# Opening stage on one load queue, small PSUM tiles in one bank, and last scalings in four products: a two-layer decoder trunk on one core

## The chip, the cores and the metric

One core of a Trainium2 chip runs the whole program. TensorE multiplies matrices and writes PSUM (8 banks), VectorE and ScalarE do elementwise work and reductions, GpSimd and SyncE here only issue DMAs; each engine works through its own queue in order. Sixteen DMA engines move the data. The metric is device time in microseconds of one execution; lower is better.

## What is computed

```python
def reference(x, c, ...):                       # x (1, 256, 1024), c (1, 1024), float32
    c_act = silu(c)
    for l in range(2):
        mod = c_act @ w_ada[l] + b_ada[l]       # nine vectors: sh0, sc0, g0, sh1, sc1, g1, sh2, sc2, g2
        h = rmsnorm(x, norm_g[l, 0]) * (1 + sc0) + sh0
        x = x + 0.5 * g0 * swiglu(h, ffn_w_gate[l, 0], ffn_w_up[l, 0], ffn_w_down[l, 0])   # 1024 -> 2816 -> 1024
        h = rmsnorm(x, norm_g[l, 1]) * (1 + sc1) + sh1
        x = x + g1 * token_mix(h, ...)          # gated MLP over chunks | differential attention | sparse attention
        h = rmsnorm(x, norm_g[l, 2]) * (1 + sc2) + sh2
        x = x + 0.5 * g2 * swiglu(h, ffn_w_gate[l, 1], ffn_w_up[l, 1], ffn_w_down[l, 1])
    return rmsnorm(x, final_g)
```

## The kernel before

All activations stay on the chip, transposed: `xT` holds 8 chunks (`KD`) of 128 features by 256 tokens. Every weight is used once and streamed from DRAM in float32. A product is made of three: each weight tile (`load`, L203, into the five buffers `wst`) is split into `wh` (ScalarE, L211) and `wl` = rest (VectorE, L215), each activation into a high and a low half, and TensorE (`mm`, L223) adds wh*high, wh*low and wl*high.

**The modulation vectors** come from `w_ada`: each `ast` tile (512 KB, four buffers `ad`) is multiplied by silu(c) (`crow`) and summed along its row by one VectorE instruction (L192 in `ada_sum`; L381 in the opening). GpSimd issues these loads (L181 in `ada_load`; L374), ahead of the stage that needs the vector.

**The opening** (`startup`, L363) is the first half-FFN's norm and its first seven gate and up tiles, with the loop over the 8 chunks k outside: for each k it loads and splits 1792 columns of weights in two parts (1024 and 768, `first`), makes this k's two modulation columns from two `ast` tiles (`ada_sum0`, L381 to L385), makes the chunk h[k] (`h_chunk`, L274: L276 VectorE, L279 ScalarE high half, L280 VectorE low half), and runs 42 products into seven PSUM banks `ps_fst`. Up to the first `h[0]` the order on TensorE, VectorE and ScalarE is written by hand (`manual_schedule`); the loop behind it is ordered by a planner that takes ready instructions by program order. The rest of the constant tables (`cst[:, P:]`, `par[:, npar0:]`, L443 and L444) and a small weight `w2` (L581) wait for no buffer.

**FFNs** (`ffn`, L447) run gate and up tiles in turn, then 8 down tiles. **The mixer** (`mix`, L547) issues its steps in the order of `MIX_ORDER`, by hand on TensorE alone; the step `a` of layer 0 sums two `ast` tiles and loads two more. `xs_in` (L591) holds both banks of pool `psw` for the token-major projections; `ws_in` (L323) takes its bank from `psw` too. The pool `pst` has one bank: `ps_cs` (compressed scores), `ps_ct` (their transposes), `ps_da` and the norm's sums take it in turn.

**The end**: after the last down tile the norm's factor per token is spread over partitions in PSUM (`rp`), eight VectorE instructions scale a chunk each by `final_g` and `rp` (L1036), and SyncE stores each (L1038).

Of the kernel before, what the change touches and what calls it, by code (L numbers as in the profile page):

```python
# [17 lines left out]
P = 128  # L18
# [32 lines left out]
k.1 dp.0 dp.1 ds.0 c.0 dx.0 k.0 ds.1 dx.1 c.1 v dr.0 q.0 ch dr.1 ns.0 a co do.0 do.1 nx.0 a cs.0 dn q.1 a q.2 go df ns.1  # L51
ct.0 nr.0 nx.1 a w.0.0.4 cs.2 no.0 q.3 a ns.2 nx.2 nr.1 ct.2 a cs.1 ns.3 nx.3 nr.2 cs.3 a ct.1 no.1 no.2 a nr.3 w.1.0.6
# [60 lines left out]
def trunk_kernel(ctx: ExitStack, tc: tile.TileContext, A, depth=DEPTH, nf=NF, fsplit=FSPLIT):  # L113
# [58 lines left out]
    last_wl = [None]  # L172
# [30 lines left out]
    def load(src, cols, pool=wst, tag="wst"):  # L203
        st = pool.tile([P, cols], F32, name="wst", tag=tag)
        nc.sync.dma_start(st, src)
        return st

    def split(src, cols, mid=None):
        st = load(src, cols)
        wh = whp.tile([P, cols], F32R, name="wh", tag="wh")  # L210
        nc.scalar.activation(wh, st, AF.Copy)  # L211
        if mid:
            mid()
# [114 lines left out]

    def add_out(l, s, m, ps, nxt, halves):
# [33 lines left out]
    def startup(ns):  # L363
# [3 lines left out]
        nc.gpsimd.dma_start(crow, A["crow"])  # L367
        b1 = sm.tile([P, KD], F32, name="b1", tag="b1", bufs=1)

        def ada_load0(k):  # L370
            sts = []
            for m in (1, 0):
                st = adp.tile([P, D], F32, name="ast", tag="ast")
                nc.gpsimd.dma_start(st, A["w_ada"][0, m, k])  # L374
                sts.append(st)
            return sts

        def ada_sum0(k, sts):
# [8 lines left out]
        def first(k, mid=None):  # L387
            parts = []
            for f0, f1 in ((0, (ns + 1) // 2), ((ns + 1) // 2, ns)):
                if f1 > f0:  # L390
                    src = A["w_first"][k, :, f0 * 2 * P:f1 * 2 * P]
                    parts.append((f0, f1, *split(src, 2 * (f1 - f0) * P, None if f0 else mid)))
            return parts

        with tc.manual_schedule(engines={mybir.EngineType.PE, mybir.EngineType.DVE, mybir.EngineType.Activation}):
# [8 lines left out]
            dma(cst[:, :P], A["cst"][:, :P])  # L404
            nc.vector.tensor_scalar_add(b1, lp(0, "bada")[:, KD:2 * KD], 1.0)
# [14 lines left out]
            ada_sum0(0, sts)  # L420
            rb = rms_bcast(rsqrt_tokens(st), in_psum=True)
            parts = first(0, lambda: h_chunk(0, 0, 0, rb))
        pss = []
        for f in range(ns):
            pool_, tag = (psm, "mm") if f < 5 else (psw, "w")
            pss.append(pool_.tile([P, 2 * T], F32, name="ps_fst", tag=tag))
        for k in range(KD):
            if k:
                parts = first(k)
            if k + 1 < KD:  # L430
                ada_sum0(k + 1, ada_load0(k + 1))
                h_chunk(0, 0, k + 1, rb)
            for f0, f1, wh, wl in parts:
                tiles = [(pss[f][:, e * T:(e + 1) * T], 2 * (f - f0) + e) for f in range(f0, f1) for e in range(2)]
                step = len(tiles) if k == 0 else 1
                for n0 in range(0, len(tiles), step):
                    for o, n in tiles[n0:n0 + step]:
                        s = slice(n * P, (n + 1) * P)
# [696 lines left out]
```

## Time and profile before

| | us |
|---|---|
| median of 3 runs | 1076.78 (1075.27 to 1077.12) |
| the profiled execution | 1076.35 |
| its span in the trace | 1074.4 |
| TensorE busy | 1028.0 |
| VectorE busy | 849.0 |
| ScalarE busy | 576.3 |

The span runs from the first to the last record of the execution; 1.95 us of the profiled execution's time lie around it. A busy time adds up an engine's instructions. TensorE's is modelled: its instructions overlap, so a busy stretch may still run slower than another, at a lower granted clock for example.

### The profile page before, as it was taken

To read this page: it belongs to the slowest core of one execution; us is meant where nothing else is said; L and a number is where in the kernel's file an instruction comes from. 1 tells how busy PE (TensorE), PEld (TensorE's weight loads), DVE (VectorE), ACT (ScalarE), POOL (GpSimd) and SP (SyncE) were. 2 spreads that over 40 slices of the span, in tenths; PEclk is the share of its full clock that TensorE was granted. 3 is DMA by queue.
4 is the path that set the end of the run, shared out by engine and by line. 5 is a ranking of instruction groups with operands and counts; after the bars stand their busy time and mean duration, and the time that the engine had idled before them with its cause. 6 is when DMAs were issued, how large, how long until landed. Compare 5 with 4: busy or idle time off the path is not lost.

```text
span 1074.4 us, 19840 instructions
## 1 busy us (share of the span) xinstructions
PE 1028.0 (96%) x7684; PEld 948.5 (88%) x7684; DVE 849.0 (79%) x1589; ACT 576.3 (54%) x1022; POOL 77.7 (7%) x151
## 2 busy tenths in 40 slices
PE   7789999999898999999999999999998999999997
PEld 5689998888676999998899999889786799999986
DVE  5689989989994899965679999667987489655553
ACT  4355544565576755444565544455566676444441
POOL 2101111000100022100001111000000001000000
PEclk8899999999999999999999999999998999999999
DMA  9899998947620499986658999765632057756551
GB/s 361 301 327 328 390 365 308 366 132 249 228 95 21 157 388 408 404 274 174 192 159 308 409 408 368 249 189 176 237 133 67 1 177 299 229 181 184 170 154 40
DMA packets 73967, 258.05 MB, mean 240 GB/s; under 512 B 8337, under 2 KB 9745, under 8 KB 73873
## 3 DMA queue, kind: packets, MB, share of 16 engines
q1 hardware_dynamic: 52560, 180.17, 48.7%
q0 software_dynamic: 20880, 76.03, 19.0%
q8 instruction: 60, 0.98, 0.4%
q10 hardware_dynamic: 432, 0.58, 0.2%
q14 instruction: 35, 0.28, 0.1%
HBM read 255.70 MB, written 1.05 MB: 239 GB/s over the span
## 4 chain that ended last, share of the span: by engine, by line
PE 77%; DVE 11%; DMA 6%; ACT 3%; issue 2%; POOL 0%; DVEq 0%; ACTq 0%; POOLq 0%; SPq 0%
PE ps_ws L223 42%; PE ps_dn L223 23%; PE ps_out L223 4%; PE ps_wu L223 4%; DVE wl L215 3%; DMA ast<-in_w_ada_dram 2%; PE ps_y L223 1%; DMA wst<-in_w_first_dram 1%; PE ps_s L223 1%; ACT pn L541 1%; DVE rt L515 1%; DVE mx L536 1%; DMA wst<-in_w_in_vs_dram 1%; ACT wh L211 1%; DVE h L280 1%
## 5 line engine op out<-in xcount | busy, mean ns | idle before, releaser
L211 ACT ACTIVATE wh<-wst 128x1024 fp32r<-128x1024 f32 (+2 forms) x332 | 342.0, 1032 | 360.7 <-issue 129.7
L215 DVE TENSOR_TENSOR wl<-wst,wh 128x1024 fp32r<-128x1024 f32 (+2 forms) x332 | 392.6, 1187 | 117.6 <-ACT wh L211 115.7
L223 PE MATMUL ps_ws<-h,wh 128*128 128x256 f32 x2720 | 481.3, 281 | 4.0 <-DVE dv L655 1.7
L223 PEld LDWEIGHTS ps_ws<-h,wh 128*128 128x128 f32 x2720 | 416.3, 189 | 7.4 <-DVE dv L655 2.5
L223 PE MATMUL ps_ws<-h,wl 128*128 128x256 f32 x1360 | 382.0, 281 | 0.0
L223 PEld LDWEIGHTS ps_ws<-h,wl 128*128 128x128 f32 x1360 | 261.1, 192 | 0.0
L223 PE MATMUL ps_dn<-act,wh 128*128 128x512 f32 (+1 forms) x726 | 247.9, 390 | 0.0
L223 PE MATMUL ps_dn<-act,wl 128*128 128x256 f32 x704 | 197.6, 281 | 0.0
L223 PEld LDWEIGHTS ps_dn<-act,wh 128*128 128x128 f32 x726 | 134.8, 188 | 30.8
L192 DVE SCALAR_TENSOR_TENSOR ast<-ast,crow 128x1024 f32<-128x1024 f32 x128 | 156.8, 1226 | 1.6 <-DMA ast<-in_w_ada_dram 1.6
L223 PEld LDWEIGHTS ps_dn<-act,wl 128*128 128x128 f32 x704 | 133.1, 189 | 0.0
L181 POOL DMA_DIRECT2D ast<-in_w_ada_dram x128 | 68.0, 531 | 465.3 <-DVE ast L192 144.2
L223 PE MATMUL ps_wu<-ut,wh 128*128 128x258 f32 (+1 forms) x320 | 60.1, 286 | 0.8 <-DVE ut L294 0.8
L223 PE MATMUL ps_fst<-h,wh 128*128 128x256 f32 x224 | 42.1, 300 | 12.6 <-ACT h L279 12.6
L223 PEld LDWEIGHTS ps_wu<-ut,wh 128*128 128x128 f32 x320 | 49.9, 189 | 1.4 <-DVE ut L294 1.3
L223 PEld LDWEIGHTS ps_fst<-h,wh 128*128 128x128 f32 x224 | 36.5, 208 | 14.1 <-ACT h L279 13.8
L223 PE MATMUL ps_out<-y,wh 128*128 128x256 f32 x256 | 47.3, 286 | 0.4 <-DVE xT L332 0.4
L219 ACT ACTIVATE act<-a 128x256 fp32r<-128x256 f32 x88 | 35.6, 412 | 18.3 <-DVE a L349 17.0
L223 PE MATMUL ps_wu<-ut,wl 128*128 128x258 f32 x160 | 45.2, 283 | 0.0
L349 DVE TENSOR_TENSOR a<-ps_ws,sg 128x256 f32<-128x256 f32 x75 | 32.0, 427 | 14.8 <-PE ps_ws L223 14.8
L223 PEld LDWEIGHTS ps_out<-y,wh 128*128 128x128 f32 x256 | 39.8, 191 | 2.0 <-issue 1.0
L332 DVE SCALAR_TENSOR_TENSOR xT<-ps_dn,hg,xT 128x256 f32<-128x256 f32 x63 | 30.4, 482 | 12.6 <-PE ps_dn L223 11.5
(202 smaller groups left out, 1033.0 us busy)
## 6 DMA issues: line engine op xcount, KB each, us to landing
ast<-in_w_ada_dram POOLq DMA_DIRECT2D x144, 512.0 KB, 7.1
wst<-in_w_gate_dram SPq DMA_DIRECT2D x81, 512.0 KB, 5.7
wst<-in_w_up_dram SPq DMA_DIRECT2D x81, 512.0 KB, 6.0
wst<-in_w_down_dram SPq DMA_DIRECT2D x64, 512.0 KB, 4.4
wst<-in_w_in_ws_dram SPq DMA_DIRECT2D x28, 512.0 KB, 4.3
wst<-in_w_down_dram SPq DMA_DIRECT2D x32, 384.0 KB, 3.5
wst<-in_cmp_w_dram SPq DMA_DIRECT2D x16, 512.0 KB, 6.3
wst<-in_w_out_dram SPq DMA_DIRECT2D x16, 512.0 KB, 3.6
```

The source lines that it names most:

```text
L181: nc.gpsimd.dma_start(st, A["w_ada"][l, m, c])
L192: nc.vector.scalar_tensor_tensor(out=st, in0=st, scalar=1.0, in1=crow, op0=ALU.mult, op1=ALU.mult, accum_out=reds[l, m][:, c:c + 1])
L211: nc.scalar.activation(wh, st, AF.Copy)
L215: last_wl[0] = nc.vector.tensor_sub(wl, st, wh.bitcast(F32))
L219: nc.scalar.activation(dst[:, :T], src, AF.Copy)
L223: nc.tensor.matmul(out, lhsT, rhs, start=start, stop=stop, skip_group_check=True)
L280: nc.vector.scalar_tensor_tensor(out=h[:, k, T:], in0=t, scalar=sh, in1=h[:, k, :T].bitcast(F32), op0=ALU.add, op1=ALU.subtract)
L332: nc.vector.scalar_tensor_tensor(out=xT[:, m, :], in0=ps[:, half * T:(half + 1) * T], scalar=hg[l][:, s, m:m + 1], in1=xT[:, m, :], op0=AL ...
L349: nc.vector.tensor_mul(a, pu, sg)
L515: nc.vector.tensor_mul(out, z, t)
L536: nc.vector.tensor_reduce(mx[:, :n], ps, axis=AX.X, op=ALU.max, negate=True)
L541: nc.scalar.activation(pt[:, g * w:(g + 1) * w], ps[:, g, :], AF.Exp, bias=mx[:, g:g + 1], accum_out=su[:, g:g + 1])
```

## The change

In the opening, all loads but two chunks of `xT` and the first constants go out on SyncE's queue in the order of use: x, c, then for each k its two `ast` tiles and its weights, one k ahead. The rest of the tables is queued behind the last weight of the opening (`issue_after`), `w2` and `wsT` behind the last down weight, and two casts (`identb`, `negb`) behind the FFN's last `wl`. x times the norm's factor (`xr`) is made two chunks at a time on VectorE; the two modulation columns and both steps up to h[k] move to ScalarE (`h_first`); the order by hand covers the whole loop on TensorE, VectorE and ScalarE. In the mixer of layer 0 the eight sums over `ast` move from the steps `a` to three places ahead of the attention steps, four loads at a time; `ps_cs`, `ps_ct` and `ps_da` become column ranges of one PSUM tile (`small`), with two ranges for `ps_cs`; the first `ws_in` behind an `xs_in` takes its bank from `psm`. At the end x times `final_g` is made by ScalarE as each chunk is finished (`fin`), four VectorE products of 512 columns multiply by `rp`, and two of the four stores go out on ScalarE's queue.

```diff
+        if nxt is None:                                    # add_out, last FFN
+            if m % 2 == 0:
+                fin.append(up.tile([P, 2, T], F32, name="fin", tag="u"))
+            nc.scalar.activation(fin[-1][:, m % 2], xT[:, m, :], AF.Copy, scale=fing[:, m:m + 1])
...
-        nc.gpsimd.dma_start(crow, A["crow"])
+        dma(cst[:, :P], A["cst"][:, :P])
+        dma(crow, A["crow"])
...
-                nc.gpsimd.dma_start(st, A["w_ada"][0, m, k])
+                dma(st, A["w_ada"][0, m, k])
...
-            nc.vector.scalar_tensor_tensor(out=gs[0][:, 0, k:k + 1], in0=red[:, 0:1], scalar=b1[:, k:k + 1],
-                                           in1=lp(0, "ng")[:, k:k + 1], op0=ALU.add, op1=ALU.mult)
-            nc.vector.tensor_add(mod[0][:, 0, k:k + 1], red[:, 1:2], lp(0, "bada")[:, k:k + 1])
...
+        def h_first(k, red):
+            nc.scalar.activation(gs[0][:, 0, k:k + 1], red[:, 0:1], AF.Identity, scale=lp(0, "ng")[:, k:k + 1],
+                                 bias=gb[:, k:k + 1])
+            nc.scalar.activation(mod[0][:, 0, k:k + 1], red[:, 1:2], AF.Identity, bias=lp(0, "bada")[:, k:k + 1])
+            t = tp.tile([P, T], F32, name="tn", tag="t1k")
+            nc.scalar.activation(t, xr[k // 2][:, k % 2], AF.Identity, scale=gs[0][:, 0, k:k + 1], bias=mod[0][:, 0, k:k + 1])
+            nc.scalar.activation(h[:, k, :T], t, AF.Copy)
+            nc.vector.tensor_sub(h[:, k, T:], t, h[:, k, :T].bitcast(F32))
+        def xr_pair(n, rp):
+            t = up.tile([P, 2, T], F32, name="xr", tag="u")
+            nc.vector.tensor_mul(t, xT[:, 2 * n:2 * n + 2], rp[:, None, :].to_broadcast([P, 2, T]))
+            xr.append(t)
...
+            for k in range(KD):
+                f0, f1, st0 = raw[0]
+                wh, wl = split_raw(st0, 2 * (f1 - f0) * P)
+                parts = [(f0, f1, wh, wl)]
+                h_first(k, red)
+                for f0, f1, st0 in raw[1:]:
+                    parts.append((f0, f1, *split_raw(st0, 2 * (f1 - f0) * P)))
+                if k + 1 < KD:
+                    raw = first_load(k + 1)
+                    if k % 2 == 0 and k // 2 + 1 < KD // 2:
+                        xr_pair(k // 2 + 1, rp)
+                    red = ada_sum0(k + 1, sts)
+                    if k + 2 < KD:
+                        sts = ada_load0(k + 2)
...
+        with tc.issue_after(last_ld[0].ins):
+            dma(cst[:, P:], A["cst"][:, P:])
+            dma(par[:, npar0:], A["par"][:, npar0:])
...
     def mix(l, ada, nxt):
+        ada_sum(len(loaded))
+        ada_load(4)
         pse = [ws_u(WI[l, 0])]
...
         early += [apply_r(ws_u(WI[l, n]), rb) for n in (12, 13)]
-        ada_sum(len(loaded))
+        ada_sum(4)
+        ada_load(4)
+        small = [pst.tile([P, 512], F32, name="ps_small", tag="st")]
...
+        def ws_next(n):                                    # behind_xs[0] = 1 at the end of xs_in
+            behind_xs[0] -= 1
+            return ws_in(WI[l, n], psm, "mm") if behind_xs[0] >= 0 else ws_in(WI[l, n])
...
         lam_exp(gelu)
+        ada_sum(4)
...
-            ps = pst.tile([P, 60], F32, name="ps_cs", tag="st")
+            ps = small[0][:, 256 + (j % 2) * 64:316 + (j % 2) * 64]
...
-            ps = pst.tile([P, T], F32, name="ps_ct", tag="st")
+            ps = small[0][:, :T]
...
-    for k in range(KD):
-        o = tp.tile([P, T], F32, name="o", tag="t1k")
-        nc.vector.scalar_tensor_tensor(out=o, in0=xT[:, k, :], scalar=fing[:, k:k + 1], in1=rp,
-                                       op0=ALU.mult, op1=ALU.mult)
-        nc.sync.dma_start(A["out"][k], o)
+    for n, (xf, queue) in enumerate(zip(fin, (nc.sync, nc.scalar) * 2)):
+        nc.vector.tensor_mul(xf, xf, rp[:, None, :].to_broadcast([P, 2, T]))
+        queue.dma_start(A["out"][2 * n:2 * n + 2].rearrange("k p t -> p k t"), xf)
```

## Rows read from the trace of the kernel before

**Rows 1.** The page of the kernel before, parts 1 and 2: TensorE's busy time, and the granted TensorE clock of 40 equal slices of 26.9 us, in tenths.
```profile
PE 1028.0 (96%) x7684; PEld 948.5 (88%) x7684; DVE 849.0 (79%) x1589; ACT 576.3 (54%) x1022; POOL 77.7 (7%) x151
...
PEclk8899999999999999999999999999998999999999
```

**Rows 2.** What TensorE waited for over the whole span (the view of waits): who waited, for whom: us in total, times, longest.
```profile
PE ps_fst L223 <- ACT h L279: 12.6, 5, 8.0
...
PE ps_s L223 <- DVE qn L525: 2.2, 1, 2.2
...
PE ps_cs L223 <- ACT pct L887: 1.7, 2, 1.3
PE ps_ws L223 <- DVE dv L655: 1.7, 1, 1.7
...
PE ps_ct L885 <- DVE ce L867: 1.3, 2, 0.7
```

**Rows 3.** The tile `ps_fst`, the products of the opening, on TensorE: duration min/median/max in ns, first and last start in us.
```profile
L223 PE MATMUL ps_fst<-h,wl x112: 276/276/415, 21.8 to 71.6; 128*128 128x256 f32 x112
```

**Rows 4.** The chain that ended last, in order of time, in the first 130 us: start, us, what.
```profile
24.39 11.34 DMA wst<-in_w_first_dram
...
37.34 5.34 PE ps_fst L223 x26
...
73.20 56.84 PE ps_ws L223 x499
```

**Rows 5.** Busy time of the engines in stretches of 5 us of the opening: length, then each engine's busy us (instructions), the granted TensorE clock, DMA share, GB/s.
```profile
0.00:5.00 5.00, 3.75 (x11) 1.47 (x12) 0.36 (x3) 1.64 (x3) 2.96 (x9) 1.00 0.54 146
...
10.00:15.00 5.00, 2.66 (x18) 2.44 (x17) 3.10 (x8) 1.90 (x4) 0.99 (x2) 0.61 1.03 416
...
30.00:35.00 5.00, 0.00 (x0) 0.00 (x0) 2.10 (x3) 2.39 (x3) 0.53 (x1) 0.66 1.03 405
35.00:40.00 5.00, 2.65 (x12) 2.66 (x13) 2.67 (x6) 2.30 (x3) 0.53 (x1) 0.50 0.52 208
...
45.00:50.00 5.00, 5.00 (x45) 5.00 (x44) 5.00 (x11) 1.77 (x3) 0.54 (x1) 1.00 0.81 266
```

**Rows 6.** DMA issues of the first 80 us: queue that issues, count, KB each, median us from issue to landing.
```profile
ast<-in_w_ada_dram POOLq DMA_DIRECT2D x20, 512.0 KB, 6.9
wst<-in_w_first_dram SPq DMA_DIRECT2D x8, 512.0 KB, 9.7
...
cst<-in_cst_dram SPq DMA_DIRECT2D x1, 706.0 KB, 17.6
...
w<-in_cmp_w_dram SPq DMA_DIRECT2D x1, 192.0 KB, 11.5
```

**Rows 7.** DMA issues of SyncE in order of time: start, us, line, out<-in, count.
```profile
2.12 4.46 SPq L205 DMA_DIRECT2D wst<-in_w_first_dram  x5
6.62 0.45 SPq L443 DMA_DIRECT2D cst<-in_cst_dram  x1
```

**Rows 8.** VectorE in order of time in the opening: start, us, line, operation, out<-in, shapes, count, and in brackets the idle time before it and its releaser.
```profile
8.93 0.23 DVE L1020 CAST identb<-cst 128x128 bf16<-128x128 f32 x1 [3.74 <-DMA cst<-in_cst_dram]
9.07 1.29 DVE L412 TENSOR_TENSOR sq<-xT 128x512 f32<-128x512 f32 x2
...
46.01 1.22 DVE L215 TENSOR_TENSOR wl<-wst,wh 128x1024 fp32r<-128x1024 f32 x1
...
47.54 0.95 DVE L215 TENSOR_TENSOR wl<-wst,wh 128x768 fp32r<-128x768 f32 x1
48.41 1.22 DVE L381 SCALAR_TENSOR_TENSOR ast<-ast,crow 128x1024 f32<-128x1024 f32 x1
...
49.55 0.48 DVE L280 SCALAR_TENSOR_TENSOR h<-tn,mod,h 128x256 fp32r<-128x256 f32 x1
...
51.29 1.22 DVE L215 TENSOR_TENSOR wl<-wst,wh 128x1024 fp32r<-128x1024 f32 x1
```

**Rows 9.** ScalarE in order of time in the opening, same columns.
```profile
8.13 1.06 ACT L417 ACTIVATE crow<-crow 128x1024 f32<-128x1024 f32 x1 [1.51 <-DMA crow<-in_crow_dram]
...
10.49 0.20 ACT L419 ACTIVATE warm<-ones 128x1 f32<-128x1 f32 x1
...
17.10 0.51 ACT L279 ACTIVATE h<-tn,mod 128x256 fp32r<-128x256 f32 x1 [3.62 <-DVE tn L276]
...
33.73 0.84 ACT L211 ACTIVATE wh<-wst 128x768 fp32r<-128x768 f32 x1 [1.20 <-DMA wst<-in_w_first_dram]
```

**Rows 10.** VectorE in order of time in layer 0's mixer: two of the eight sums over `ast` there, the last of them among them.
```profile
277.65 1.23 DVE L192 SCALAR_TENSOR_TENSOR ast<-ast,crow 128x1024 f32<-128x1024 f32 x1 [0.65 <-DMA ast<-in_w_ada_dram]
...
291.45 1.21 DVE L192 SCALAR_TENSOR_TENSOR ast<-ast,crow 128x1024 f32<-128x1024 f32 x1
```

**Rows 11.** Busy time of the engines in two stretches of 20 us of layer 0's mixer: length, then each engine's busy us (instructions), the granted TensorE clock, DMA share, GB/s.
```profile
220.00:240.00 20.00, 20.00 (x123) 17.70 (x122) 17.25 (x45) 13.18 (x21) 0.00 (x0) 1.00 0.28 89
...
280.00:300.00 20.00, 16.64 (x105) 13.48 (x104) 18.95 (x50) 9.42 (x27) 0.53 (x1) 0.83 0.56 182
```

**Rows 12.** All engines in order of time at the end of the span.
```profile
1067.84 3.22 DVE L1036 SCALAR_TENSOR_TENSOR o<-xT,par,rp 128x256 f32<-128x256 f32 x8 [0.53 <-PE rp L264]
1068.35 3.77 SPq L1038 DMA_DIRECT2D out_dram<-o  x8
```

**Rows 13.** The busy times of the engines while the result is stored, columns as in the stretches above.
```profile
1070.00:1072.00 2.00, 0.00 (x0) 0.00 (x0) 1.06 (x3) 0.00 (x0) 0.00 (x0) 0.50 0.79 267
```

More of the change, by code (lines that the diff above doesn't have):

```diff
@@ L171, in trunk_kernel @@
     todo, loaded, reds, done = [], [], {}, set()
-    last_wl = [None]
+    last_wl, last_ld = [None], [None]
     def ada_load(n, after=None):
@@ L327, in ws_in @@
         return ps
+    fin = []
     def add_out(l, s, m, ps, nxt, halves):
@@ L373, in ada_load0, with first_load @@
                 st = adp.tile([P, D], F32, name="ast", tag="ast")
-                nc.gpsimd.dma_start(st, A["w_ada"][0, m, k])
+                dma(st, A["w_ada"][0, m, k])
                 sts.append(st)
             return sts
+        def first_load(k):
+            return [(f0, f1, load(A["w_first"][k, :, f0 * 2 * P:f1 * 2 * P], 2 * (f1 - f0) * P))
+                    for f0, f1 in ((0, (ns + 1) // 2), ((ns + 1) // 2, ns)) if f1 > f0]
         def ada_sum0(k, sts):
@@ L382, in ada_sum0 @@
                                                accum_out=red[:, n:n + 1])
-            nc.vector.scalar_tensor_tensor(out=gs[0][:, 0, k:k + 1], in0=red[:, 0:1], scalar=b1[:, k:k + 1],
-                                           in1=lp(0, "ng")[:, k:k + 1], op0=ALU.add, op1=ALU.mult)
-            nc.vector.tensor_add(mod[0][:, 0, k:k + 1], red[:, 1:2], lp(0, "bada")[:, k:k + 1])
[L387 to L393, printed above, removed]
+            return red
+        def h_first(k, red):
[10 more added lines that the diff above has]
+            xr.append(t)
+        xr = []
         with tc.manual_schedule(engines={mybir.EngineType.PE, mybir.EngineType.DVE, mybir.EngineType.Activation}):
@@ L419, in startup @@
             nc.scalar.activation(warm, ones, AF.Sqrt)
[L420 to L426, printed above, removed]
-        for k in range(KD):
[L428 to L438, printed above, removed]
-                        mm(o, wh[:, s], h[:, k, :T], start=(k == 0 and n % 2 == 0), stop=False)
-                        mm(o, wh[:, s], h[:, k, T:], start=False, stop=False)
-                    for o, n in tiles[n0:n0 + step]:
-                        mm(o, wl[:, n * P:(n + 1) * P], h[:, k, :T], start=False, stop=(k == KD - 1))
@@ L443, in startup @@
-        dma(cst[:, P:], A["cst"][:, P:])
-        dma(par[:, npar0:], A["par"][:, npar0:])
+            red = ada_sum0(0, sts)
+            rp = rms_bcast(rsqrt_tokens(st), in_psum=True)
+            xr_pair(0, rp)
+            sts = ada_load0(1)
+            pss = []
+            for f in range(ns):
+                pool_, tag = (psm, "mm") if f < 5 else (psw, "w")
+                pss.append(pool_.tile([P, 2 * T], F32, name="ps_fst", tag=tag))
+            for k in range(KD):
[12 more added lines that the diff above has]
+                        sts = ada_load0(k + 2)
+                for f0, f1, wh, wl in parts:
+                    tiles = [(pss[f][:, e * T:(e + 1) * T], 2 * (f - f0) + e) for f in range(f0, f1) for e in range(2)]
+                    for wx, hs, first_, last_ in ((wh, slice(0, T), True, False), (wh, slice(T, 2 * T), False, False),
+                                                  (wl, slice(0, T), False, True)):
+                        for o, n in tiles:
+                            mm(o, wx[:, n * P:(n + 1) * P], h[:, k, hs], start=(first_ and k == 0 and n % 2 == 0),
+                               stop=(last_ and k == KD - 1))
@@ L739, in da_norm @@
         def da_norm():
-            dst = pst.tile([P, 8], F32, name="ps_da", tag="st")
+            dst = small[0][:, 384:392]
             for a in range(2):
@@ L1019, in trunk_kernel @@
             ffn(l, 0, [(l, m) for m in (2, 4, 3, 5, 7)], (l, 1))
-            nc.vector.tensor_copy(identb, ident)
-            nc.vector.tensor_copy(negb, cs("neg"))
+            with tc.issue_after(last_wl[0].ins):
+                nc.vector.tensor_copy(identb, ident)
+                nc.vector.tensor_copy(negb, cs("neg"))
             with tc.manual_schedule(engines={mybir.EngineType.PE}):
```

40 lines of the change are left out of this document (21 added, 19 removed).

## The prediction

> **What bounds the kernel now.** I read the page first, then the view of waits, then the chain in order of time. TensorE is busy 1028.0 of 1074.4 us, and its granted clock is full in nearly every slice; the first two and a late one are not [rows 1]. So a gain can only come from where TensorE stands or runs at its lower clock. The waits say where: of the 46.4 us that it stands, 12.6 are products of the opening that wait for h, one of them 8.0 us; the mixers' are smaller: 2.2 us for a query tile, 1.7 and 1.3 us for `ps_cs` and `ps_ct`, 1.7 us for the first product behind the token-major projection [rows 2].
>
> The opening runs until the last `ps_fst` product, begun at 71.6, is done at 71.9 us [rows 3]. The chain shows why it is long: a weight load issued at 24.4 takes 11.34 us, and at 37.34 TensorE starts again; from 73.20 on, the chain is TensorE without a break [rows 4]. Between 30 and 35 TensorE does nothing while the DMA engines are full at 405 GB/s; behind the hole it runs at clock 0.50, the lower level; warm, 45 products fit into 5 us, 0.111 us each [rows 5]. What filled the DMA engines was not all wanted: the rest of `cst` (706 KB) and `w2` (192 KB) are among the loads of that time, beside `ast` tiles loaded ahead [rows 6]. SyncE had put `cst` right behind the first five weights, at 6.62 [rows 7]. The opening is bound by the order of its loads, the rest by TensorE.
>
> **The opening, start.** Up to the first pair of sums the new queue carries x (1.05 MB), the first constants and parameters (0.12), c (0.52) and a pair of `ast` tiles (1.05): 2.74 MB. At 146 GB/s in the first 5 us and 416 GB/s then [rows 5] the pair has landed at 5 + (2.74 - 0.73)/0.416 = 9.8 us. VectorE's two squares (1.29) began at 9.07 behind a cast that waited for `cst` [rows 8]; that cast is gone, and the squares end by 9.3. c is there at 7.4 and its silu, 1.06 on ScalarE [rows 9], done by then. Two sums at 1.15 (the pitch of L381) end at 11.6 at the earliest. Reciprocal, transposes, the first `xr` pair (half of the two squares, 0.65) and small waits: 1.6 us, an estimate; two steps on ScalarE at 0.51 [rows 8, 9]: first product at 14.2.
>
> **The opening, one k.** VectorE has no idle time now from one `wl` at 46.01 to the next at 51.29: 5.28 us [rows 8]. After the change, from the end of a k's sums: two small ScalarE steps, of which one latency (0.20) counts, two of 0.51 in turn, 0.04 of signals: h at +1.25. Meanwhile VectorE makes the first `wl` (1.14) and then the low half (0.40). ScalarE goes on with the second `wh`, 0.84, VectorE with its `wl`, 0.87, then the next k's sums, 2.3. The period is 1.25 + 0.84 + 0.87 + 2.3 = 5.26 us, with 0.65 more in every second k for `xr` [rows 8, 9]. TensorE's 42 products take 42 x 0.111 = 4.7 and wait a little in each k.
>
> Is the queue fast enough? A k needs 1.97 MB, 4.7 us at 416 GB/s. SyncE stands at the `ast` tiles of k+2 until the sums of k are done, and the weights of k+2 queue behind them. Its issues cost 4.46/5 = 0.89 us under load [rows 7], four of them 3.6 us. With 6.9 us to landing [rows 6] the second tile is there 7.8 us after those sums; it is wanted two periods less one sum later, at 9.4. So VectorE keeps the pace.
>
> The Trainium skill, "DMA: Bandwidth & Descriptors", section "Bandwidth", puts a core's share of HBM at about 358 GB/s; the trace disagrees, with 416 GB/s over 5 us [rows 5]. By the page's figure a k would take 5.5 us and the forecast would rise by an estimated 1.5 us.
>
> **The opening, sum.** The sums for k=1 end at 18.85 (14.2, less the 1.0 of the two steps; then VectorE: `wl` 1.14, low half 0.40, a wait for `wh`, `wl`, `xr`, sums), h[1] comes at 20.1, h[7] at 20.1 + 6 x 5.26 + 2 x 0.65 = 53.0, and 4.7 us of products end the stage at 57.7 in place of 71.9: **-14.2 us**. Bounds: if TensorE sets the pace, 14.2 + 1.9 (an estimate for the lower clock at the start; behind the hole it lasts from 37.34 to beyond 40 [rows 4, 5]) + 8 x 4.7 = 53.7, -18.2; if only the 8.0 us hole and its 2 us of lower clock go, -10. What follows is TensorE-bound, so it moves forward whole. The 1.4 MB put behind the opening's loads are first read in the mixer, and are covered by the FFN between.
>
> **The mixers.** (a) The wait of 1.7 us for `dv` copies [rows 2] goes with the other bank; a wait for the next rope step may take part of it: -1.3 (0 to -1.7). (b) One bank in turn costs 1.7 + 1.3 us [rows 2] over both layers. These are in stretches where VectorE's own order follows close behind: half, -1.5 (0 to -3.0). (c) Eight sums at 1.14 (9.2 us) leave the attention steps, where the last ones still stand in VectorE's queue at 277.65, with a DMA wait, and at 291.45 [rows 10]. With them may go the 2.2 us wait for the query tile [rows 2] and part of the lower clock (0.83 over 280 to 300, that is 6.8 us at the lower level; with products in half of that, 1.7 us lost [rows 11]). I take half, -2.0 (0 to -3.9). They come back ahead of the attention steps, where VectorE is busy 17.25 of 20 us and DMA is idle (share 0.28) [rows 11]. The nearest rows give 0 (the planner finds all of it a gap) to +6.4 (9.2 less the idle 2.75 of that stretch); I take +1.0, because TensorE is some tiles of `wl` behind VectorE there. While the eight tiles hold the four `ad` buffers, the compression weights queue on SyncE behind them, and the projection weights behind those; they are wanted some 15 us later. Sum **-3.8** (+6.4 to -8.6).
>
> **The end.** Eight scalings take 3.22 us and SyncE's eight issues 3.77, 0.47 each, ending last [rows 12]. Four products at 0.65 take 2.6; two issues on each of two queues lie beside them, and the last is issued about 0.9 us sooner; a store is twice as big, +0.1. **-0.8** (0 to -1.3). The eight new ScalarE copies lie beside TensorE's down tiles; the last fits between the square and the root, else it costs 0.4.
>
> The Trainium skill, "DMA: Bandwidth & Descriptors", section "Rules for kernel authors", speaks against the second queue: spreading DMAs over issuing engines brings no bandwidth and saves only issue time. In these rows the DMA engines are 0.79 busy at 267 GB/s [rows 13], so issue time is what is short, in the rule's own terms. Were bandwidth the limit, the end would give an estimated -0.2 and the forecast 0.6 more.
>
> The rest costs nothing: casts and small loads queued later lie beside FFN work.
>
> **Sum.** -14.2 - 3.8 - 0.8 = -18.8 us. The profiled execution took 1076.35, its span 1074.4 and 1.95 around it, 0.4 under the median of 1076.78. 1076.35 - 18.8 = **1057.5 us**.
>
> **Rivals.**
> - *The sums bite where they now stand.* VectorE, near full ahead of the attention steps, delays the `wl` tiles; (c) is +6.4, (a) nothing, (b) as taken. 1076.35 - 14.2 + 4.9 - 0.8 = 1066.3. For it: 17.25 of 20 busy [rows 11]; against: TensorE hardly waits for VectorE there [rows 2].
> - *TensorE paces the opening, and the mixers give their most.* VectorE's own work in a k is only 4.7 us without its two waits. -18.2, (a) and (b) in full, (c) at -1.8, and -0.8: 1050.9. Against: the sums must end before h can start, by the written order.
> - *Slower: one queue lands late.* With landing time L the period is (0.9 + L + 1.15)/2, as the pair of k+2 waits for the sums of k. At the median 6.9 this does not bind. At the 17.6 us of `cst` [rows 6] it is 9.8: the opening ends at 20.1 + 6 x 9.8 + 4.7 = 83.6, +11.7, and the total is 1083.5. It turns the whole slower from a period of about 9, L = 16. Against: 17.6 was the fate of one load behind everybody else's.
> - *The order does not hold on SyncE*, which is not ordered by hand: other loads slip between, and only the hole goes, -10: 1061.7.
>
> **How the numbers follow.** Forecast 0.60; sums bite 0.15; TensorE paces 0.13; late queue 0.04; order lost 0.08. The range reaches from just under the second rival to just over the first, 1049.5 to 1066.5; the rest of those two and the late queue lie outside. A measurement of this kernel tells about 0.2% (2.2 us) from no change. Faster 0.95; same 0.02 and slower 0.03 come from the late queue and from a mixer worse than bounded.
>
> **What would show it.** Right: `ps_fst` starts near 14 and ends near 58; no hole over 1.5 us in it; clock full from about 19; VectorE's period 5.3 to 5.9; `cst` issued behind the last opening weight. Sums over `ast` before 260 and no TensorE wait for a query tile near 268; no waits for `ps_ct` or `ps_cs` on their bank. Four products and four stores at the end, 0.8 us shorter. Wrong: `ast` landing over 9 us in the opening, TensorE holes in 205 to 245 that wait for `wl`, or a chain that leaves TensorE in the first FFN.

## The result, and the profile after

The changed kernel takes 1065.69 us in the median of four runs (1063.18 to 1067.39), the kernel before beside it 1076.03: ratio 0.9899, 95% interval 0.9874 to 0.9924. That is 10.3 us less. It lies inside the predicted range (1049.5 to 1066.5), 8.2 over the forecast of 1057.5 and 0.8 under the range's upper end. Run again, the same kernel took 1062.23, ratio 0.9851 (0.9821 to 0.9881). Its first profiled execution, from which the rows here come, was the fastest of its four: 1063.18, span 1061.4, 13.0 under the span before.

Where the 13.0 come from is read from the order of TensorE's instructions, by the first or last product of each stage (us). The last column is the version that the experiments end with. "The tables" are the rest of the constant tables, `cst` and `par`.

| stage mark | before | changed | tables moved, second profile |
|---|---|---|---|
| first `ps_fst` | 17.66 | 15.31 | 15.19 |
| `ps_fst` ends | 71.88 | 60.18 | 60.04 |
| first `ps_dn` | 154.93 | 146.05 | 141.50 |
| layer 0's mixer, first `ps_wu` | 215.94 | 207.07 | 202.52 |
| the FFN behind it, first `ps_wu` | 361.79 | 351.15 | 344.72 |
| layer 1's mixer, first `ps_wu` | 737.32 | 726.66 | 720.28 |
| the FFN behind it, first `ps_wu` | 877.02 | 864.32 | 860.90 |
| last `ps_dn` ends | 1065.18 | 1052.46 | 1049.06 |
| span | 1074.4 | 1061.4 | 1058.0 |

The differences before to changed: opening -11.7 at its end; **2.8 given back** up to the first `ps_dn` (83.05 us before, 85.87 now); mixers -1.8 and -2.0; all FFN stages behind the first within 0.03 us of before; from the last down product to the span's end 9.22 before, 8.94 now, -0.3.

The opening, by stretches of 5 us (columns as in [rows 5]):
```profile
10.00:15.00 5.00, 0.92 (x5) 0.43 (x4) 4.09 (x7) 3.76 (x8) 0.00 (x0) 0.69 1.03 415
...
20.00:25.00 5.00, 5.00 (x45) 5.00 (x44) 4.38 (x6) 3.41 (x6) 0.00 (x0) 1.00 1.02 403
45.00:50.00 5.00, 4.62 (x40) 4.42 (x40) 4.69 (x7) 2.96 (x6) 1.19 (x2) 1.00 0.95 316
55.00:60.00 5.00, 4.88 (x42) 4.86 (x42) 3.42 (x11) 3.55 (x8) 0.00 (x0) 1.00 1.03 412
60.00:65.00 5.00, 2.72 (x14) 2.34 (x13) 3.54 (x5) 3.30 (x6) 0.00 (x0) 0.81 0.97 368
65.00:70.00 5.00, 5.00 (x39) 5.00 (x39) 4.32 (x4) 4.31 (x6) 0.00 (x0) 0.85 0.85 278
```
The hole of 30 to 35 us before is gone and the clock is full from 20 on. But behind the stage, in 60 to 65, TensorE stands again (busy 2.72 of 5 us), and for some of 60 to 70 it has its lower clock, where before it worked at full clock. The load queue kept up. From issue to landing, `ast` tiles take 6.1 us and weights 7.0 and 7.5 (before 6.9 and 9.7, [rows 6]):
```profile
ast<-in_w_ada_dram SPq DMA_DIRECT2D x16, 512.0 KB, 6.1
wst<-in_w_first_dram SPq DMA_DIRECT2D x8, 512.0 KB, 7.0
...
wst<-in_w_first_dram SPq DMA_DIRECT2D x8, 384.0 KB, 7.5
```
One k in VectorE's order, with the making of two chunks of `xr` in it (columns as in [rows 8]):
```profile
36.68 1.22 DVE L215 TENSOR_TENSOR wl<-wst,wh 128x1024 fp32r<-128x1024 f32 x1
38.21 0.42 DVE L404 TENSOR_TENSOR h<-tn,h 128x256 fp32r<-128x256 f32 x1 [0.31 <-ACT h L403]
38.94 0.96 DVE L215 TENSOR_TENSOR wl<-wst,wh 128x768 fp32r<-128x768 f32 x1 [0.31 <-ACT wh L213]
39.82 0.68 DVE L408 TENSOR_TENSOR xr<-xT,rp 128x512 f32<-128x512 f32 x1
...
42.71 1.22 DVE L215 TENSOR_TENSOR wl<-wst,wh 128x1024 fp32r<-128x1024 f32 x1
```
From 36.68 to 42.71 is 6.03 us; the next k, without `xr`, takes 5.43 (to 48.14). The opening's first product waited for the first sums over `ast`, which waited for the first `ast` tile:
```profile
10.13 1.23 DVE L392 SCALAR_TENSOR_TENSOR ast<-ast,crow 128x1024 f32<-128x1024 f32 x1 [2.00 <-DMA ast<-in_w_ada_dram]
```

The end, all engines (compare [rows 12]), and two microseconds of it with the DMA engines' share and GB/s in the last two columns:
```profile
1055.12 2.48 DVE L1076 TENSOR_TENSOR fin<-fin,rp 128x512 f32<-128x512 f32 x4 [0.52 <-PE rp L264]
1055.84 1.63 SPq L1077 DMA_DIRECT2D out_dram<-fin  x2
1056.50 1.59 ACTq L1077 DMA_DIRECT2D out_dram<-fin  x2
```
```profile
1057.00:1059.00 2.00, 0.00 (x0) 0.00 (x0) 0.60 (x2) 0.00 (x0) 0.00 (x0) 0.50 1.01 341
```
The four issues take 1.63 and 1.59 us on their two queues, in place of 3.77 on one, and are over by 1058.1; the DMA engines are full from 1057 to 1059, at 341 GB/s.

### The profile page after: what moved, and what is told of

The parts are those of the page before. It is cut to its first block, busy times and chain, and to the rows that moved or that the text cites. A ratio compares the mean times of both kernels' runs of the same rounds, so it can differ in the third digit from the quotient of the medians.

```text
span 1061.4 us, 19845 instructions
## 1 busy us (share of the span) xinstructions
PE 1024.9 (97%) x7684; PEld 946.4 (89%) x7684; DVE 847.0 (80%) x1565; ACT 587.8 (55%) x1054; POOL 68.8 (6%) x134
## 4 chain that ended last, share of the span: by engine, by line
PE 75%; DVE 15%; ACT 4%; DMA 4%; issue 2%; DVEq 0%; SPq 0%; ACTq 0%
PE ps_ws L223 41%; PE ps_dn L223 21%; PE ps_out L223 4%; PE ps_wu L223 4%; DVE wl L215 3%; DVE rt L544 2%; DMA wst<-in_w_first_dram 2%; PE ps_s L223 1%; DVE ast L192 1%; DVE mx L565 1%; DMA wst<-in_w_up_dram 1%; PE ps_y L223 1%; ACT pn L570 1%; DVE ast L392 1%; ACT wh L213 1%
## 5 line engine op out<-in xcount | busy, mean ns | idle before, releaser
L334 DVE SCALAR_TENSOR_TENSOR xT<-ps_dn,hg,xT 128x256 f32<-128x256 f32 x63 | 30.3, 481 | 12.5 <-PE ps_dn L223 11.5
L220 DVE TENSOR_TENSOR act<-a,act 128x256 fp32r<-128x256 f32 x88 | 36.1, 417 | 0.6 <-ACT act L219 0.5
L223 PE MATMUL ps_out<-y,wl 128*128 128x256 f32 x128 | 36.2, 283 | 0.0
```

The lines of the kernel that those rows point to most:

```text
L220: nc.vector.tensor_sub(dst[:, T:], src, dst[:, :T].bitcast(F32))
L223: nc.tensor.matmul(out, lhsT, rhs, start=start, stop=stop, skip_group_check=True)
L334: nc.vector.scalar_tensor_tensor(out=xT[:, m, :], in0=ps[:, half * T:(half + 1) * T], scalar=hg[l][:, s, m:m + 1], in1=xT[:, m, :], op0=AL ...
```

## The experiments

**The gap behind the opening.** First the kernel itself again, then three edits, all on one chip.

> The changed kernel once more, nothing edited, to see what differs between its executions (its four times so far lie 4.2 us apart, those of the kernel before 2.4). Theory (the weights behind the opening come late and TensorE's clock falls there): the opening's products end at 60.2 +-0.5 in every trace, and the start of the first down tile, 146.05 in the first trace, moves by up to 3 us with the hole behind the opening. Rival (the spread comes from somewhere else, the mixers say): the first down tile starts within 0.5 us of 146.05, and the spread lies behind it.

Measured 1062.23 (ratio 0.9851); `ps_fst` 15.00 to 59.85, first `ps_dn` 145.51, mixers 142.5 and 138.9. The 85.66 us from the opening's end to the first `ps_dn` are there again (85.87 in the first profile), so the two executions differ behind it, in the mixers: the rival, but for 0.04 us. A later profile with the same opening, that of the stores on one queue, shows that this stretch can differ too: the hole is there (1.50 + 0.65 us), the clock stays full (1.00 in 60 to 70), and the first `ps_dn` starts 84.15 behind the opening's end. So the lower clock is some 1.6 us of the stretch.

```diff
-        with tc.issue_after(last_ld[0].ins):          # in startup, behind the opening
-            dma(cst[:, P:], A["cst"][:, P:])
-            dma(par[:, npar0:], A["par"][:, npar0:])
+            if l == 0 and w == 0 and f == f0 + 4:     # in ffn, at the fifth gate and up tile
+                with tc.issue_after(last_ld[0].ins):
+                    nc.sync.dma_start(cst[:, P:], A["cst"][:, P:])
+                    nc.sync.dma_start(par[:, npar0:], A["par"][:, npar0:])
```


> The rest of the two constant tables (1.2 MB) is queued behind the loads of gate and up tile 11 in place of the last opening weight. Theory (what the opening gained is partly given back because the tables and the next stage's modulation tiles stand in front of the first gate and up weights): 1.2 MB at 410 GB/s is 2.9 us, so the hole behind the opening (1.5 + 0.8 us and about 2 us of lower clock) shrinks to under 1 us and the first down tile starts at 143 to 144.5 in place of 146.05; the whole -1.5 to -2.8. Rival (ScalarE and VectorE are late with the splits, not the DMA): the same times as now.

Measured 1060.92, ratio 0.9833 (0.9798 to 0.9867). `ps_fst` ends at 60.36, the next products run on without a hole, the clock stays full, and the first `ps_dn` starts at 141.83: 81.47 us behind the opening's end, 4.4 less than in the changed kernel. So the whole loss of 2.8 there is bought back, and 1.6 more than that.

```diff
             act = [None] * len(raw)
+            seen = sm.tile([P, 1], F32, name="seen", tag="seen", bufs=1)
+            gate_ = nc.gpsimd.tensor_copy(seen, raw[-1][:, 0:1])     # GpSimd's ast loads start later
```


> GpSimd's loads of modulation tiles for the next stage wait until the last product of the opening's tiles is taken out of PSUM (a one-column copy on GpSimd); now the first four (2.1 MB) are issued between 47 and 54 us. Theory (as for the tables): 2.1 MB at 410 GB/s is 5.1 us, so the first gate and up weights are early enough, the hole behind the opening is under 1 us, and the first down tile starts at 143 to 144.5; the whole -1.5 to -2.8. Rival (splits are late, not the DMA): the same as now, or up to 2 us more where the held tiles are then missed at tile 11.

Measured 1064.67, ratio 0.9879 (0.9844 to 0.9914). The first part of the hole is as long as ever, 1.51 us, and the second 0.45 in place of 0.77, while the DMA engines are only half used in 60 to 65 (share 0.51, 163 GB/s). This run corrects the theory of the one before it. ScalarE in order of time, first in the changed kernel:
```profile
57.49 1.22 ACT L350 ACTIVATE sg<-ps_fst 128x256 f32<-128x256 f32 x4 [0.39 <-PE ps_fst L223]
59.76 0.94 ACT L350 ACTIVATE sg<-ps_fst 128x256 f32<-128x256 f32 x3 [1.05 <-PE ps_fst L223]
60.57 1.07 ACT L213 ACTIVATE wh<-wst 128x1024 fp32r<-128x1024 f32 x1
61.85 1.06 ACT L213 ACTIVATE wh<-wst 128x1024 fp32r<-128x1024 f32 x1 [0.21 <-DMA wst<-in_w_up_dram]
```
then with GpSimd's loads later:
```profile
59.79 0.94 ACT L350 ACTIVATE sg<-ps_fst 128x256 f32<-128x256 f32 x3 [1.05 <-PE ps_fst L223]
60.60 4.86 ACT L213 ACTIVATE wh<-wst 128x1024 fp32r<-128x1024 f32 x5
```
and with the tables moved:
```profile
55.17 2.73 ACT L213 ACTIVATE wh<-wst 128x768 fp32r<-128x768 f32 x3
57.91 1.28 ACT L350 ACT_TABLE_LOAD   x1
59.21 2.04 ACT L350 ACTIVATE sg<-ps_fst 128x256 f32<-128x256 f32 x7
```
In the middle rows five `wh` follow each other with no DMA wait, so the weights were there; still the first `wh` of the FFN begins at 60.60. It stands in ScalarE's queue behind the seven `sg`, which wait for the opening's last products. With the tables moved the planner writes the other order: two of the FFN's `wh` go ahead of `sg` (x3 from 55.17, one of them still the opening's).

In the changed kernel itself the late weight holds TensorE just as long. Its chain that ended last goes through the landing of the first `up` tile, 12.44 us after its issue:
```profile
49.38 12.44 DMA wst<-in_w_up_dram
...
62.96 83.25 PE ps_ws L223 x718
```
It landed at 61.82, its `wh` was made by 62.92, and at 62.96 TensorE went on. With that weight there in time and the order as it was, TensorE went on at 62.66 (GpSimd's loads later). So two things hold TensorE here, to within 0.3 us of each other: the weight lands late, and its split is queued late. The order is enough for the hole by itself, as this run shows; whether the late landing would be enough too, under the other order, no run shows. Moving the tables takes both away.

```diff
-                f0, f1, st0 = raw[0]
-                wh, wl = split_raw(st0, 2 * (f1 - f0) * P)
-                parts = [(f0, f1, wh, wl)]
+                parts = [(f0, f1, *split_raw(st0, 2 * (f1 - f0) * P)) for f0, f1, st0 in raw]
                 h_first(k, red)
-                for f0, f1, st0 in raw[1:]:
-                    parts.append((f0, f1, *split_raw(st0, 2 * (f1 - f0) * P)))
```


> In each k of the opening both weight parts are split before h is made, so that ScalarE's second wh no longer stands behind h. Theory (VectorE's written order sets the period, 5.42 and 6.03 us, of which 0.31 + 0.31 are waits for h and for the second wh, and 0.4 the second wl that now fills the wait for h): VectorE's period falls to 4.7 and 5.3, the opening's products end at 55.5 to 57 in place of 60.2; but the DMA then has to bring 1.97 MB in 4.85 us, all it can, so the weights behind the opening come no sooner and the hole there grows by as much: the first down tile starts at 145 to 146.5, the whole -1 to +0.5. Rival (TensorE or the DMA sets the period already): the opening ends at 60.2 +-0.5.

Measured 1062.28, ratio 0.9843 (0.9804 to 0.9882), as the repeat. `ps_fst` ends at 56.41, 3.8 sooner; the hole grows to 1.63 + 1.59, with a clock of 0.66 from 60 to 65, and the first `ps_dn` is at 146.33. `sg` ahead of `wh` costs the first 1.63, and the second `wh` waits 1.03 for its landing. This profile and the one before it ran the stretch behind at a slower pace at full clock, 3.2 us in all (last section); less that, the first `ps_dn` would be at 143.1, an estimate, so a part of the 3.8 is kept. How much is not settled.

Both edits together:

> The tables are issued in the middle of the first FFN, and beside that ScalarE makes the wh of both parts ahead of the h of each round. Theory (the gain of the shorter opening was given back only because the FFN's first weights landed late behind the tables): both gains now add up; ps_fst ends near 56.5 as with the wh ahead alone, ps_ws follows within 0.5 us, and the first ps_dn starts 3 to 4 us ahead of that with the tables moved alone (141.8), at 138 to 139; total about 3.5 below the tables alone. Rival (the FFN's first weights are paced by the DMA engines themselves, which carry the opening's weights until its end): ps_fst ends near 56.5, a hole of 2 to 4 us stands behind it without the tables, and the first ps_dn starts at 141 to 142 again.

Measured 1061.93, ratio 0.9847 (0.9809 to 0.9885), first `ps_dn` 142.10: the rival's time. The mechanism is neither's, it is the order on ScalarE once more, the other way round:
```profile
50.79 0.60 ACT L402 ACTIVATE tn<-xr,mod,gs 128x256 f32<-128x256 f32 x1
52.01 1.06 ACT L213 ACTIVATE wh<-wst 128x1024 fp32r<-128x1024 f32 x1 [0.61 <-DMA wst<-in_w_gate_dram]
52.97 0.40 ACT L403 ACTIVATE h<-tn 128x256 fp32r<-128x256 f32 x1
```
The FFN's `wh` has slipped between the last k's `tn` and its `h`, and waits for its weights; TensorE stands 2.07 us for that h (51.35 to 53.42). `ps_fst` ends at 58.98, and a third `wh`, waiting until 57.11 ahead of `sg`, puts off `sg` and, with it, the product on VectorE that TensorE waits for: a hole of 1.40 behind the opening.

**Is it the holding back of the tables that shortens the opening?** The `issue_after` around the two loads is taken away, their place in the program kept:

```diff
-        with tc.issue_after(last_ld[0].ins):
-            dma(cst[:, P:], A["cst"][:, P:])
-            dma(par[:, npar0:], A["par"][:, npar0:])
+        dma(cst[:, P:], A["cst"][:, P:])
+        dma(par[:, npar0:], A["par"][:, npar0:])
```

> As the changed kernel, but the rest of the tables is not held behind the opening's last weights. Theory (the DMA engines are full in the opening, so what goes ahead of the weights delays them by its own length): 1.2 MB at about 410 GB/s is 2.9 us, ps_fst ends 2.5 to 3 later (62.7 to 63.1), the hole behind it is gone or under 0.5, and the first ps_dn starts where it did, 145 to 146. Rival (holding does nothing, the two loads stand last in the queue in any case): ps_fst ends within 0.5 of the changed kernel's 60.2, with the same hole of 1.5.

Measured 1065.94, ratio 0.9898 (0.9867 to 0.9929), `ps_fst` 15.30 to 60.17, the hole 1.5, first `ps_dn` 145.82: the rival. The two loads are issued at 44.33 and 44.81 with the hold and without it, behind the opening's last weight; their place in the queue's program order is enough. No run takes the other edits of the opening apart.

**The mixers.** Both mixers and their order as before, opening and end as changed (the diff of the change, turned round in `MIX_ORDER` and `mix` but for the two loads behind the last down weight):

> Opening and end as in the changed kernel; both mixers and their order as before (ada steps back, no other bank behind xs, no shared small bank). Theory: the mixers' part of the gain is 3.8 us, 1.8 in layer 0 and 2.0 in layer 1 by the distance from the first ps_wu of a mixer to that of the following FFN (144.1 and 137.7 in the changed kernel, 145.9 and 139.7 here). Rival (the mixers gain nothing by themselves, they only stood at another granted clock in the two profiled executions): both distances stay within 0.5 of the changed kernel's.

Measured 1066.50, ratio 0.9892 (0.9857 to 0.9926); mixers 145.4 and 140.0, together 285.4, as before (285.55). Over all nine profiles in which the mixers are the changed ones their sum lies between 279.7 and 282.8. So the part is worth 2.6 to 5.7 us by these profiles, with the theory's 3.8 among them. Next, the shared tile alone undone: `ps_cs`, `ps_ct` and `ps_da` are tiles of their own again. (The expectations call this "its own bank"; there is one bank in `pst` in either kernel, and the tiles take it in turn.)

```diff
-        small = [pst.tile([P, 512], F32, name="ps_small", tag="st")]
...
-            dst = small[0][:, 384:392]
+            dst = pst.tile([P, 8], F32, name="ps_da", tag="st")
...
-            ps = small[0][:, 256 + (j % 2) * 64:316 + (j % 2) * 64]
+            ps = pst.tile([P, 60], F32, name="ps_cs", tag="st")
...
-            ps = small[0][:, :T]
+            ps = pst.tile([P, T], F32, name="ps_ct", tag="st")
```

> Each small group has its own bank again, the rest as in the changed kernel. The prediction gave the shared bank 1.5 us (bounds 0 to 3.0). Theory now: nothing, since the waits on pct and ce are the same in both profiled kernels (0.46 and 0.72 in layer 0, 1.3 and 0.6 in layer 1): both mixers keep their length to 0.4 us. Rival (the prediction's step): the mixers grow by 1.5 together and the waits on ps_st's release come back.

Measured 1063.62, ratio 0.9864 (0.9828 to 0.9899); mixers 146.1 and 139.3, 3.7 longer than in the changed kernel, though TensorE's gaps in them add up to 16.8 us against 18.2. The length is in the granted clock: in layer 1 it falls behind the short `ps_cs` and `ps_da` products, where it stayed full in all seven profiles with the shared tile up to then. I took this for a real gain of the shared tile and tested it on the better kernel with the same diff, beside a repeat of that kernel:

> The same kernel as the one with the tables moved alone, timed in more rounds and profiled once more. If its gain over the changed kernel is real: 3 to 5 us below the changed kernel's median, so 0.983 to 0.985 of the kernel before; no hole behind the opening; both mixers as long as there (142.2 and 137.6, to 1.0). If the first profile of it was a lucky execution: within 2 us of the changed kernel, 0.987 or above.

> The tables moved, and each small group in its own bank again. Theory, from the three profiles with own banks against the six with the shared one: in layer 1 the granted clock falls to 0.50 for some 3.5 us behind the short products ps_cs and ps_da, 74 to 80 us into the mixer, and that mixer is 1.7 longer than in the same kernel with the shared bank (139.3 against 137.6), with the same waits. Rival (the clock fell there in three profiles by chance, and the shared bank does nothing): layer 1's mixer within 0.4 of the same kernel with the shared bank, and no time at 0.50 at that place.

The repeat took 1059.81 (ratio 0.9846, 0.9820 to 0.9871), without the shared tile 1061.33 (0.9853, 0.9828 to 0.9877). My theory fell in both: the repeat, which has the shared tile, has the lower clock at that place, and its twin without it has not. TensorE in the same 5 us of layer 1's mixer (busy us and products, granted clock, DMA share, GB/s), the tables moved, second profile:
```profile
794.28:799.28 5.00, 5.00 (x29) 0.66 0.02 3
```
and without the shared tile:
```profile
798.63:803.63 5.00, 4.75 (x34) 1.00 0.02 5
```
Layer 1's mixer took 137.58 in the first and 140.62 in the second profile of one and the same kernel. A group of three products that takes 0.64 us at the lower clock (804.34 to 804.98 below) takes 0.34 at the full one (801.55 to 801.89 in the changed kernel):
```profile
804.34 0.41 PE L223 MATMUL ps_ws<-h,wl 128*128 128x256 f32 x1
804.56 0.63 PE L223 MATMUL ps_ws<-h,wh 128*128 128x256 f32 x2
804.98 0.41 PE L223 MATMUL ps_ws<-h,wl 128*128 128x256 f32 x1
```
(these rows are from the changed kernel without the shared tile). What the lower clock costs, worked out as TensorE's busy time times one minus the granted clock and summed over stretches of 2 us, comes in pieces of about 1.6 us, two to six of them in a profile's two mixers: 3.1 us in the first profile with the tables moved, 4.6 in the changed kernel, 6.5 before, 9.6 with the shared tile undone. Less these pieces the mixers take 275.8 and 276.2 without the shared tile and 276.5 to 279.2 with it. That subtraction is rough, since a wait behind a piece can take it back: layer 0's mixer takes 144.1 to 144.6 us in three profiles with a piece some 27 us in and one at 68, and 144.2 to 144.6 in three with the one at 68 alone. Where layer 1 has its pieces at the same places, the shared tile makes little difference: 138.9 with it against 139.1, and 139.1 against 139.3. So it shortens no wait, and no stage by more than some 0.3 us, that these runs can show.

The sums over `ast` back between the steps, on the better kernel:

```diff
-        ada_sum(len(loaded))                  # ahead of the first ws_u
-        ada_load(4)
...
-        ada_sum(4)                            # behind the early ws_u; and once more behind lam_exp
-        ada_load(4)
+        ada_sum(len(loaded))
...
+            "a": ada_step,                    # ada_sum(2), ada_load(2); eight a in layer 0's MIX_ORDER, as before
```

> The tables moved, and the mixer's ada sums back in steps of two between the other steps; the other bank behind xs and the shared small bank stay. Theory (the three sums put together ahead of wl cost in layer 0 what the other bank saved, as VectorE had no free stretch there): the wait of 1.8 us for wl 25 us into layer 0 is gone, the lower clock behind it too, and layer 0's mixer is 1.5 to 2.5 shorter than with the sums together (142.2), less what comes back at the query tiles (up to 1.0). Rival (the prediction's step: the sums in the late steps cost 2.0, and moving them gained 1.0 net): layer 0's mixer 1.0 longer, 143.2 or more, with a wait of 2.0 at the query tiles.

Measured 1062.40, ratio 0.9862 (0.9836 to 0.9888). The wait for `wl` is gone, as my theory said, but layer 0's mixer takes 142.9, longer than the 142.2 that it was to shorten, with one piece of lower clock in either: what comes back is 0.62 for a weight's landing (`cmp_w`), 0.92 and 0.83 for VectorE. Theory fallen; of the prediction's net gain of 1.0 for the move, 0.7 is here (142.9 against 142.2). The query tile is waited for 1.14 us, as in the changed kernel, so it is not the sums that made that wait. The wait for `wl`, in the changed kernel, VectorE and then TensorE:
```profile
228.59 1.22 DVE L192 SCALAR_TENSOR_TENSOR ast<-ast,crow 128x1024 f32<-128x1024 f32 x1
...
230.88 1.22 DVE L192 SCALAR_TENSOR_TENSOR ast<-ast,crow 128x1024 f32<-128x1024 f32 x1
...
232.43 1.22 DVE L215 TENSOR_TENSOR wl<-wst,wh 128x1024 fp32r<-128x1024 f32 x1
```
```profile
231.45 0.40 PE L223 MATMUL ps_ws<-h,wh 128*128 128x256 f32 x2
233.70 0.53 PE L223 MATMUL ps_ws<-h,wl 128*128 128x256 f32 x1 [1.86 <-DVE wl L215]
```
The other bank let TensorE go on at 231.45; three sums of 1.15 us had just gone in front of the `wl` that it wants next.

**The end**, all four stores on SyncE:

```diff
-    for n, (xf, queue) in enumerate(zip(fin, (nc.sync, nc.scalar) * 2)):
+    for n, (xf, queue) in enumerate(zip(fin, (nc.sync, nc.sync) * 2)):
```

> All four stores on SyncE, the products as in the changed kernel. Theory (the bytes set the end: the DMA engines are full from the second store on): from the last down product's end to the span's end as in the changed kernel, 9.0 us, to 0.3. Rival (the prediction's: issue time on SyncE sets it): the last two stores are issued behind the first two, about 1.6 us later each, and the end comes 0.8 to 1.6 later.

Measured 1061.94, ratio 0.9853 (0.9814 to 0.9891). From the last down product to the span's end 8.96 us, against 8.94 in the changed kernel: the second queue brings nothing. Four issues on one queue take 2.20 us, no more than the two queues' 2.25 from the first issue to the last one's end, and are over before the data is out:
```profile
1054.54 2.20 SPq L1077 DMA_DIRECT2D out_dram<-fin  x4
```
```profile
1055.70:1057.70 2.00, 0.00 (x0) 0.00 (x0) 0.60 (x2) 0.00 (x0) 0.00 (x0) 0.50 1.01 339
```

**The version to keep** is the one with the tables moved: 0.9833 and 0.9846 of the kernel before on two chips, 1.3 us under the changed kernel on the one chip and 6.1 under the twin of it without the hold on the other. The intervals overlap the changed kernel's, so the times alone do not show the gain; the trace carries the claim. The first `ps_dn` starts at 141.5 and 141.8 in its two profiles, against 144.5 to 146.1 in the six profiles of the changed kernel's opening, with the hold or without it.

## Why the prediction was right or wrong

- **The number.** Of the 8.2 us over the forecast, some 2.5 are the opening's size, 2.8 what was given back behind it and 0.5 the end; the other 2.5 lie between the profiled execution and the median of four. The median is 0.6 from the time of the first rival (1066.3), whose price is not what was paid, so that the range holds it is in part luck.
- **What bounds the kernel** held: the opening is the only stage where TensorE stood for long, and nearly all FFN time is the same to 0.03 us.
- **The opening, -14.2 forecast, -11.7 measured.** The mechanism is as written: no hole, clock full from 20, VectorE's round sets the pace, SyncE's queue keeps up. The terms are off in size. The first product is at 15.31, not 14.2: the first `ast` tile let the sums begin at 10.13 and end at 12.5, against 9.3 and 11.6 (the pair was to be there by 9.8). One k takes 5.43 and 6.03 us, not 5.26 and 5.91: ScalarE's `tn` is 0.60 and `h` 0.42, and VectorE waits 0.31 twice a k. 1.1 + 1.4 us in all.
- **The failed step is "What follows is TensorE-bound, so it moves forward whole."** 2.8 us were given back at once: TensorE's hole there is 1.5 and 0.8 us (1.3 before), and the lower clock behind it, some 1.6, is new. Before, four of the FFN's `wh` stood ahead of `sg`. The hole came from the last of them, which waited for its landing and put off `sg`:
```profile
69.93 1.06 ACT L211 ACTIVATE wh<-wst 128x1024 fp32r<-128x1024 f32 x1 [3.16 <-DMA wst<-in_w_up_dram]
```
  Now all stand behind `sg`, and the first `up` weight takes 12.44 us to land. The tables "covered by the FFN between" were not free: moved, they let the weights land sooner and the planner put two `wh` first. That the order makes the hole without the bandwidth is shown by the run whose weights were there and whose hole stayed. What was not tried is the other order alone, with the tables left in place, where the weight would still land late; so how much of the 4.4 us the later tables give by themselves stays open.
- **Mixers, -3.8 forecast, -3.8 measured**, and over all profiles -2.6 to -5.7: the sum was right, its parts were not, so the agreement is luck. (a) The wait for `dv` went as said, and a wait of 1.86 for `wl` took its place in layer 0, since (c) put three sums there: the first rival's mechanism, at its place and at under a third of its price (6.4), and one of the prediction's own signs of being wrong. (b) "One bank in turn costs 1.7 + 1.3 us" was wrong in part, and the edit took neither away: TensorE still waits 0.46 and 1.34 for `pct` and 0.72 and 0.62 for `ce`, the values that [rows 2] sums for the old tiles. The wait for `ce` is for data: `ce` is what the products of `ps_ct` transpose. The wait for `pct` is for the place, as forecast: the products that wait read `kcmp` and `qn`, and `pct` is the copy of the transposes out of PSUM. In layer 0 of the changed kernel:
```profile
309.11 0.38 PE L929 MATMUL ps_small<-cst,ce 128*30 128x128 f32 x2
309.53 0.37 ACT L931 ACTIVATE pct<-ps_small 30x256 f32<-30x256 f32 x1 [0.97 <-PE ps_small L929]
309.95 0.63 PE L223 MATMUL ps_small<-kcmp,qn 128*128 128x30 f32 x4 [0.46 <-ACT pct L931]
```
  The copy reads the tile's first 256 columns and the products write others, yet they still take turns. Whether the chip or the kernel's scheduler asks for that, no run shows. (c) Net 0.7 of the 1.0; the query tile's wait fell from 2.18 to 1.14 and did not go, and it is 1.14 with the sums back too. What made the total come out is in good part the lower clock. Both profiles of the old mixers have four pieces of it, eight of the nine of the changed ones two or three, and one four; their number differs between executions of one kernel, so how far the change or chance took them away is not settled.
- **The end, -0.8 forecast, -0.3 measured.** The term was taken from issue time on the strength of [rows 13], 0.79 busy. With larger stores issued closer together the share is 1.01, so the bytes set the end, for which the prediction had -0.2. The Trainium skill, "DMA: Bandwidth & Descriptors", section "Rules for kernel authors", says that more issuing engines bring no bandwidth; the trace agrees, with 8.94 us on two queues and 8.96 on one. As for the rate of loads, the prediction took 416 GB/s for a disagreement with a core's share of 358. The Trainium skill, "HBM Reference", section "Specifications (TRN2)", says that a core streaming alone measures well above its share; the trace agrees, with 403 to 415 GB/s between 10 and 25 us.
- **Rivals.** Late queue: landings 6.1 to 7.5, far from 16. TensorE pacing the opening: refuted by the period, 5.43 and 6.03 against 4.7. Order lost on SyncE: refuted, since the tables were issued behind the opening's last weight, and not even the hold was needed.

## What to carry to other kernels

When a stage gets shorter, look at when the next stage's first loads land and at what each in-order engine has queued across the stage's end: here a weight that landed late and a split that stood behind the last stage's tail held TensorE to within 0.3 us of each other, and moving two loads took both away. Take two profiles of the same kernel before a difference of 1 to 3 us in one stage is given to an edit; compare stages by their waits and their granted clock, not by their lengths alone. Before a wait is put down to data or to a bank, compare the releaser with what the waiting instruction reads: if it reads nothing of it, it waits for the place.

## What the runs showed of the hardware

TensorE has two paces at a granted clock of 1.00. The tables moved, second profile, two stretches of FFN products of the same kind:
```profile
120.00:140.00 20.00, 20.00 (x179) 1.00 1.01 391
```
and its twin with the shared tile undone, the same opening and the same work there:
```profile
120.00:140.00 20.00, 20.00 (x172) 1.00 1.01 383
```
179 against 172 products in 20 us, 0.112 and 0.116 us each. Ten of the fourteen profiles ran the first FFN at the quicker pace and four at the slower; it makes 3.2 us from the end of `ps_fst` to the first `ps_dn` (81.46 against 84.67). In the later FFNs all fourteen have 172 or 173. The slow ones are GpSimd's loads later, the `wh` ahead, and the last two edits on top of the moved tables (shared tile undone, sums between the steps). The pace of executions without a profile is not known, so small differences of those kernels' times from the others' say little. Nothing in these runs says what sets it.

The granted clock fell to 0.50 in pieces of some 1.6 us of TensorE's busy time each, by the working above. They lie at the same few places of the mixers, most of them with short products and waits between them: in layer 0 some 27, 65 to 80 and 105 to 120 us into the mixer, in layer 1 some 75 and 90. But they do not lie at the same ones of them in two executions of one kernel.
